# RMSNorm with SiLU on one core: later stores, earlier sums, one Newton step fewer, a square moved to ScalarE, and a halved last store

## The chip, the core and the metric

The kernel runs on one core of one Trainium2 chip. The metric is the device time of the program in microseconds (us). TensorE is called PE in the profile, VectorE DVE, ScalarE ACT, GpSimd POOL and SyncE SP. A load brings data from HBM into SBUF, a store takes it back. Loads are issued on the SP queue (row q1 of the page), stores on the ACT queue (q10), and the page counts the packets of both against the same 16 DMA engines: in the kernel before, loads alone took 100.0% of their time (12.84 to 32.27 us, 432 GB/s), stores alone 100.6% (290 to 302 us, 434 GB/s), and the two mixed 50.4% and 50.0% (42 to 280 us, 433 GB/s).

## The reference

The input `x` is 8 x 1024 rows of 2048 float32, `gamma` has 2048 values.

```python
rms = np.sqrt(np.mean(x ** 2, axis=-1, keepdims=True) + eps)
out = gamma * x / rms
return (out * (1 / (1 + np.exp(-out)))).astype(np.float32)
```

67.1 MB must be read and 67.1 MB written. Nothing can be kept back.

## The kernel before

The 8192 rows are cut into 16 blocks of 128 partitions x 4 rows, 4.19 MB each. Six buffers hold one block each; the load of block b+6 goes into the buffer of block b as soon as its store has landed. A block is squared and summed (two rows on ScalarE, two on VectorE), VectorE computes 1/rms by a bit trick and four Newton steps, multiplies by gamma, and ScalarE applies Silu with 1/rms as its scale.

```python
def rsqrt(ss):
    # ... var = ss / d + eps, then the first guess y by a shift and a subtraction
    for _ in range(4):
        nc.vector.scalar_tensor_tensor(out=t, in0=y, scalar=-0.5, in1=y, op0=ALU.mult, op1=ALU.mult)
        nc.vector.tensor_mul(out=t, in0=t, in1=var)
        nc.vector.scalar_tensor_tensor(out=y, in0=t, scalar=1.5, in1=y, op0=ALU.add, op1=ALU.mult)
    return y

def work(b):
    # ... rows 0 and 1: nc.scalar.activation(Square, accum_out=...)
    # ... rows 2 and 3: nc.vector.tensor_tensor_reduce(...)
    rstd = rsqrt(ss)
    for j in range(J):
        nc.vector.tensor_mul(out=row(b, j), in0=row(b, j), in1=g)
        nc.scalar.activation(out=row(b, j), in_=row(b, j), func=ACT.Silu, scale=rstd[:, j:j + 1])
    nc.scalar.dma_start(out=ob[b], in_=blocks.pop(b))

for b in range(nblk):
    work(b)
    if b + LEAD < nblk:      # LEAD = 6
        load(b + LEAD)       # on the SP queue; waits for the store of b
```

Of the kernel before, what the change touches and what calls it, by code (L numbers as in the profile page):

```python
# [1 line left out]

# [4 lines left out]

ACT = mybir.ActivationFunctionType
ALU = mybir.AluOpType


@with_exitstack
def kernel(
    ctx: ExitStack,
    tc: tile.TileContext,
    x: bass.AP,
    gamma: bass.AP,
    eps: bass.AP,
    out: bass.AP,
):  # L20





    nc = tc.nc
    P = nc.NUM_PARTITIONS
    f32, i32 = mybir.dt.float32, mybir.dt.int32
    x2 = x.flatten_outer_dims()
    o2 = out.flatten_outer_dims()  # L30
    n, d = x2.shape
    J = 4
    BUFS, LEAD = 6, 6
    nblk = n // (P * J)
    xb = x2.rearrange("(b p j) d -> b p (j d)", p=P, j=J)
    ob = o2.rearrange("(b p j) d -> b p (j d)", p=P, j=J)

    singles = ctx.enter_context(tc.tile_pool(name="singles", bufs=1))
    pool = ctx.enter_context(tc.tile_pool(name="pool", bufs=BUFS))
    small = ctx.enter_context(tc.tile_pool(name="small", bufs=2))  # L40
    psum = ctx.enter_context(tc.tile_pool(name="psum", bufs=1, space=bass.MemoryType.PSUM))

    g = singles.tile([P, d], f32)
    ones = singles.tile([1, P], f32)
    junk_a = psum.tile([P, d], f32, name="junk_a")
    junk_v = psum.tile([P, d], f32, name="junk_v")
    blocks = {}

    def load(b):
        xt = pool.tile([P, J * d], f32, name="xt")  # L50
        nc.sync.dma_start(out=xt, in_=xb[b])
        blocks[b] = xt

    def row(b, j):
        return blocks[b][:, j * d:(j + 1) * d]

    def rsqrt(ss):


        var = small.tile([P, J], f32, name="var")  # L60
        nc.vector.tensor_scalar(out=var, in0=ss, scalar1=1.0 / d, scalar2=float(eps),  # L61
                                op0=ALU.mult, op1=ALU.add)
        y = small.tile([P, J], f32, name="y")
        t = small.tile([P, J], f32, name="t")
        nc.vector.tensor_single_scalar(out=t.bitcast(i32), in_=var.bitcast(i32), scalar=1,  # L65
                                       op=ALU.logical_shift_right)
        nc.vector.tensor_scalar(out=y.bitcast(i32), in0=t.bitcast(i32), scalar1=-1, scalar2=0x5F375A00,  # L67
                                op0=ALU.mult, op1=ALU.add)
        for _ in range(4):
            nc.vector.scalar_tensor_tensor(out=t, in0=y, scalar=-0.5, in1=y, op0=ALU.mult, op1=ALU.mult)  # L70
            nc.vector.tensor_mul(out=t, in0=t, in1=var)  # L71
            nc.vector.scalar_tensor_tensor(out=y, in0=t, scalar=1.5, in1=y, op0=ALU.add, op1=ALU.mult)  # L72
        return y

    def work(b):
        ss = small.tile([P, J], f32, name="ss")
        for j in (0, 2, 1, 3):
            if j < J // 2:
                nc.scalar.activation(out=junk_a, in_=row(b, j), func=ACT.Square,  # L79
                                     accum_out=ss[:, j:j + 1])  # L80
            else:
                nc.vector.tensor_tensor_reduce(  # L82
                    out=junk_v, in0=row(b, j), in1=row(b, j), scale=1.0, scalar=0.0,
                    op0=ALU.mult, op1=ALU.add, accum_out=ss[:, j:j + 1])
        rstd = rsqrt(ss)
        for j in range(J):
            nc.vector.tensor_mul(out=row(b, j), in0=row(b, j), in1=g)  # L87
            nc.scalar.activation(out=row(b, j), in_=row(b, j), func=ACT.Silu, scale=rstd[:, j:j + 1])  # L88
        nc.scalar.dma_start(out=ob[b], in_=blocks.pop(b))  # L89

    with tc.manual_schedule():
        grow = pool.tile([P, J * d], f32, name="xt")
        nc.scalar.dma_start(out=grow[0:1, 0:d],
                            in_=bass.AP(tensor=gamma.tensor, offset=gamma.offset, ap=[[d, 1], gamma.ap[0]]))
        for b in range(min(LEAD, BUFS - 1)):
            load(b)
        nc.vector.memset(ones, 1.0)  # L97
        for c in range(0, d, 512):
            nc.tensor.matmul(junk_v[:, c:c + 512], ones, grow[0:1, c:c + 512], start=True, stop=True)  # L99
        nc.vector.tensor_copy(out=g, in_=junk_v)  # L100
        load(BUFS - 1)
        for b in range(nblk):
            work(b)
            if b + LEAD < nblk:
                load(b + LEAD)


# [1 line left out]
_INS = ['x', 'gamma', 'eps']  # L109
_OUTS = [((8, 1024, 2048), 'float32')]  # L110

_NUMBERS = {'eps': 9.999999747378752e-06}


# [26 lines left out]
```

## Time and profile before

| | before |
|---|---|
| time, median of 4 runs | 319.52 us (319.48 to 319.63) |
| span in the profile | 317.6 us |
| VectorE / ScalarE busy | 256.8 us (81%) / 194.8 us (61%) |
| DMA, both data queues | 98.5% of 16 engines' time |
| GB/s from 42 to 303 us | 433 |

The time is some 1.8 us longer than the span from the first to the last instruction. The groups of instructions of the page (line, engine, operation, form, count | busy us, mean ns of one | idle time before them and what ended it) give the unit costs:

```profile
L87 DVE TENSOR_TENSOR xt<-xt,g 128x2048 f32<-128x2048 f32 x64 | 142.2, 2284 | 0.0
L79 ACT ACTIVATE junk_a<-xt 128x2048 f32<-128x2048 f32 x32 | 60.2, 1881 | 17.1 <-DMA xt<-in_x_dram 10.3
L61 DVE TENSOR_SCALAR var<-ss 128x4 f32<-128x4 f32 x16 | 2.7, 170 | 27.9 <-ACT junk_a L79 27.8
```

The reader is to see that every large instruction costs about 2 us (1.88 to 2.30) for one row of 128 partitions, and that VectorE waits 27.8 us in all for ScalarE's squares. The lines that show what bounds the kernel stand in the prediction.

### The profile page before, as it was taken

To read this page: it belongs to the slowest core of one execution; us is meant where nothing else is said; L and a number is where in the kernel's file an instruction comes from. 1 tells how busy PE (TensorE), PEld (TensorE's weight loads), DVE (VectorE), ACT (ScalarE), POOL (GpSimd) and SP (SyncE) were. 2 spreads that over 40 slices of the span, in tenths; PEclk is the share of its full clock that TensorE was granted. 3 is DMA by queue.
4 is the path that set the end of the run, shared out by engine and by line. 5 is a ranking of instruction groups with operands and counts; after the bars stand their busy time and mean duration, and the time that the engine had idled before them with its cause. 6 is when DMAs were issued, how large, how long until landed. Compare 5 with 4: busy or idle time off the path is not lost.

```text
span 317.6 us, 637 instructions
## 1 busy us (share of the span) xinstructions
PE 7.2 (2%) x8; PEld 2.5 (1%) x8; DVE 256.8 (81%) x370; ACT 194.8 (61%) x130; POOL 0.2 (0%) x4
## 2 busy tenths in 40 slices
PE   6200000000000000000000000000000000000000
PEld 2000000000000000000000000000000000000000
DVE  0699697997979798897979799797979979797920
ACT  1339577483848659383956838395774838486540
POOL 0000000000000000000000000000000000000000
DMA  8999999999999999999999999999999999999967
GB/s 331 421 438 446 380 429 442 414 462 404 454 413 442 438 425 450 410 454 410 446 425 438 442 421 454 404 454 421 438 437 426 446 417 446 413 450 421 438 285 330
DMA packets 4614, 134.26 MB, mean 423 GB/s; under 512 B 513, under 2 KB 513, under 8 KB 513
## 3 DMA queue, kind: packets, MB, share of 16 engines
q1 hardware_dynamic: 2304, 67.11, 49.5%
q10 hardware_dynamic: 2306, 67.12, 49.0%
q14 instruction: 4, 0.03, 0.0%
HBM read 67.12 MB, written 67.11 MB: 423 GB/s over the span
## 4 chain that ended last, share of the span: by engine, by line
DVE 58%; ACT 27%; issue 4%; DMA 4%; ACTq 2%; DVEq 1%
DVE xt L87 44%; ACT junk_a L79 17%; ACT xt L88 10%; DMA xt<-in_x_dram 4%; DVE t L70 3%; DVE t L71 3%; DVE y L72 3%; ACTq L89 2%; DVE junk_v L82 1%; DVE t L65 1%; DVE var L61 1%; DVE y L67 1%; DVEq L136 1%; DVE ss L82 0%; DVEq L61 0%
## 5 line engine op out<-in xcount | busy, mean ns | idle before, releaser
L88 ACT ACTIVATE xt<-xt,y 128x2048 f32<-128x2048 f32 x64 | 128.1, 2002 | 92.5 <-DVE xt L87 92.3
L87 DVE TENSOR_TENSOR xt<-xt,g 128x2048 f32<-128x2048 f32 x64 | 142.2, 2284 | 0.0
L82 DVE CUSTOM_DVE_ANT_0 junk_v<-xt 128x2048 f32<-128x2048 f32 x32 | 73.5, 2296 | 1.3 <-DMA xt<-in_x_dram 0.8
L79 ACT ACTIVATE junk_a<-xt 128x2048 f32<-128x2048 f32 x32 | 60.2, 1881 | 17.1 <-DMA xt<-in_x_dram 10.3
L61 DVE TENSOR_SCALAR var<-ss 128x4 f32<-128x4 f32 x16 | 2.7, 170 | 27.9 <-ACT junk_a L79 27.8
L72 DVE SCALAR_TENSOR_TENSOR y<-t,y 128x4 f32<-128x4 f32 x64 | 10.4, 162 | 2.2
L70 DVE SCALAR_TENSOR_TENSOR t<-y 128x4 f32<-128x4 f32 x64 | 10.4, 162 | 2.2
L71 DVE TENSOR_TENSOR t<-t,var 128x4 f32<-128x4 f32 x64 | 10.3, 161 | 2.2
L100 DVE COPY g<-junk_v 128x2048 f32<-128x2048 f32 x1 | 2.3, 2291 | 8.9 <-PE junk_v L99 8.9
L99 PE MATMUL junk_v<-xt,ones 1*128 1x512 f32 x8 | 7.2, 1072 | 2.7 <-DMA xt<-in_gamma_dram 2.7
L79 ACT ACTIVATION_READ_ACCUMULATOR junk_a<-xt 128x1 f32 x32 | 6.0, 186 | 0.0
L82 DVE DVE_READ_ACCUMULATOR2_ANT ss<- 128x1 f32 x32 | 4.5, 140 | 0.0
L65 DVE TENSOR_SCALAR t<-var 128x4 int32<-128x4 int32 x16 | 2.7, 170 | 0.5
L67 DVE TENSOR_SCALAR y<-t 128x4 int32<-128x4 int32 x16 | 2.7, 170 | 0.5
L99 PEld LDWEIGHTS junk_v<-xt,ones 1*128 1x128 f32 x8 | 2.5, 325 | 5.8 <-issue 5.8
L79 ACT ACT_TABLE_LOAD x1 | 1.3, 1283 | 1.3 <-PEq L122 1.3
L88 ACT ACT_TABLE_LOAD x1 | 1.3, 1283 | 0.0
L97 DVE MEMSET ones<- 1x128 f32 x1 | 0.2, 165 | 0.8 <-PEq L122 0.8
L122 POOL MEMSET const-bfloat16-1.0<- 128x1 bf16 x1 | 0.1, 102 | 0.0
L122 POOL MEMSET const-uint8-127<- 128x1 uint8 x1 | 0.1, 102 | 0.0
L122 POOL MEMSET const-float32-1.0<- 128x1 f32 x1 | 0.1, 99 | 0.0
L122 POOL MEMSET const-float32-0.0<- 128x1 f32 x1 | 0.1, 98 | 0.2 <-issue 0.2
## 6 DMA issues: line engine op xcount, KB each, us to landing
xt<-in_x_dram SPq DMA_DIRECT2D x16, 4096.0 KB, 53.1
out_dram<-xt ACTq DMA_DIRECT2D x16, 4096.0 KB, 30.7
xt<-in_gamma_dram ACTq DMA_DIRECT2D x1, 8.0 KB
```

Source lines behind the costliest of these rows:

```text
L61: nc.vector.tensor_scalar(out=var, in0=ss, scalar1=1.0 / d, scalar2=float(eps), op0=ALU.mult, op1=ALU.add)
L65: nc.vector.tensor_single_scalar(out=t.bitcast(i32), in_=var.bitcast(i32), scalar=1, op=ALU.logical_shift_right)
L67: nc.vector.tensor_scalar(out=y.bitcast(i32), in0=t.bitcast(i32), scalar1=-1, scalar2=0x5F375A00, op0=ALU.mult, op1=ALU.add)
L70: nc.vector.scalar_tensor_tensor(out=t, in0=y, scalar=-0.5, in1=y, op0=ALU.mult, op1=ALU.mult)
L71: nc.vector.tensor_mul(out=t, in0=t, in1=var)
L72: nc.vector.scalar_tensor_tensor(out=y, in0=t, scalar=1.5, in1=y, op0=ALU.add, op1=ALU.mult)
L79: nc.scalar.activation(out=junk_a, in_=row(b, j), func=ACT.Square, accum_out=ss[:, j:j + 1])
L82: nc.vector.tensor_tensor_reduce(out=junk_v, in0=row(b, j), in1=row(b, j), scale=1.0, scalar=0.0, op0=ALU.mult, op1=ALU.add, accum_out=ss[ ...
L87: nc.vector.tensor_mul(out=row(b, j), in0=row(b, j), in1=g)
L88: nc.scalar.activation(out=row(b, j), in_=row(b, j), func=ACT.Silu, scale=rstd[:, j:j + 1])
L89: nc.scalar.dma_start(out=ob[b], in_=blocks.pop(b))
L99: nc.tensor.matmul(junk_v[:, c:c + 512], ones, grow[0:1, c:c + 512], start=True, stop=True)
```

## The change

Its intent: take work off VectorE, the busiest compute engine; sum a block before the Silu of the block ahead of it, so that neither engine waits for the other; hold a store back so that loads run ahead and stores are left over to cover the arithmetic of the last block; and begin the last store when half of the block is done. Cut to its core (`...` marks cuts):

```diff
-        for _ in range(4):
+        for _ in range(3):
 ...
-    def work(b):
+    def sums(b, after_first=()):
         ss = small.tile([P, J], f32, name="ss")
-        for j in (0, 2, 1, 3):        # two rows on each engine
+        ... row J-1 by nc.vector.tensor_tensor_reduce
+        for j in range(J - 1):
+            nc.scalar.activation(out=junk_a, in_=row(b, j), func=ACT.Square,
+                                 accum_out=ss[:, j:j + 1])
+            if j == 0:
+                for s in after_first:
+                    store(s)
 ...
+    def finish(b, pieces=1):
+        ... multiply and Silu row by row; with pieces=2 a store after two rows
+    def store(b):
+        nc.scalar.dma_start(out=ob[b], in_=blocks[b])
+        if b + LEAD < nblk:
+            load(b + LEAD)
 ...
-        for b in range(nblk):
-            work(b)
-            if b + LEAD < nblk:
-                load(b + LEAD)
+        sums(0); rstds[0] = rsqrt(sss[0]); finish(0)
+        sums(1); rstds[1] = rsqrt(sss[1])
+        for b in range(1, last - 1):
+            sums(b + 1, after_first=[b - 1])
+            finish(b)
+            rstds[b + 1] = rsqrt(sss[b + 1])
+        store(last - 2); finish(last - 1); store(last - 1)
+        sums(last); rstds[last] = rsqrt(sss[last])
+        finish(last, pieces=2)
```

More of the change, by code (lines that the diff above doesn't have):

```diff
@@ L46 @@
     junk_v = psum.tile([P, d], f32, name="junk_v")
-    blocks = {}
+    blocks, sss, rstds = {}, {}, {}
     def load(b):
@@ L73, in rsqrt @@
         return y
-    def work(b):
+    def sums(b, after_first=()):
         ss = small.tile([P, J], f32, name="ss")
-        for j in (0, 2, 1, 3):
-            if j < J // 2:
-                nc.scalar.activation(out=junk_a, in_=row(b, j), func=ACT.Square,
-                                     accum_out=ss[:, j:j + 1])
-            else:
-                nc.vector.tensor_tensor_reduce(
-                    out=junk_v, in0=row(b, j), in1=row(b, j), scale=1.0, scalar=0.0,
-                    op0=ALU.mult, op1=ALU.add, accum_out=ss[:, j:j + 1])
-        rstd = rsqrt(ss)
+        nc.vector.tensor_tensor_reduce(
+            out=junk_v, in0=row(b, J - 1), in1=row(b, J - 1), scale=1.0, scalar=0.0,
+            op0=ALU.mult, op1=ALU.add, accum_out=ss[:, J - 1:J])
+        for j in range(J - 1):
[4 more added lines that the diff above has]
+                    store(s)
+        sss[b] = ss
+    def finish(b, pieces=1):
         for j in range(J):
             nc.vector.tensor_mul(out=row(b, j), in0=row(b, j), in1=g)
-            nc.scalar.activation(out=row(b, j), in_=row(b, j), func=ACT.Silu, scale=rstd[:, j:j + 1])
-        nc.scalar.dma_start(out=ob[b], in_=blocks.pop(b))
+            nc.scalar.activation(out=row(b, j), in_=row(b, j), func=ACT.Silu,
+                                 scale=rstds[b][:, j:j + 1])
+            if pieces > 1 and (j + 1) % (J // pieces) == 0:
+                w = J // pieces * d
+                i = (j + 1) // (J // pieces) - 1
+                nc.scalar.dma_start(out=ob[b][:, i * w:(i + 1) * w], in_=blocks[b][:, i * w:(i + 1) * w])
+    def store(b):
+        nc.scalar.dma_start(out=ob[b], in_=blocks[b])
+        if b + LEAD < nblk:
+            load(b + LEAD)
     with tc.manual_schedule():
@@ L101 @@
         load(BUFS - 1)
-        for b in range(nblk):
-            work(b)
-            if b + LEAD < nblk:
-                load(b + LEAD)
+        last = nblk - 1
+        sums(0)
+        rstds[0] = rsqrt(sss[0])
+        finish(0)
+        sums(1)
+        rstds[1] = rsqrt(sss[1])
+        for b in range(1, last - 1):
+            sums(b + 1, after_first=[b - 1])
+            finish(b)
+            rstds[b + 1] = rsqrt(sss[b + 1])
+        store(last - 2)
+        finish(last - 1)
+        store(last - 1)
+        sums(last)
+        rstds[last] = rsqrt(sss[last])
+        finish(last, pieces=2)
 _INS = ['x', 'gamma', 'eps']
```

## The prediction

> **What bounds the kernel now.** I read the page's engine shares first, then the slices and the DMA part.
>
> ```profile
> PE 7.2 (2%) x8; PEld 2.5 (1%) x8; DVE 256.8 (81%) x370; ACT 194.8 (61%) x130; POOL 0.2 (0%) x4
> ...
> DMA  8999999999999999999999999999999999999967
> ...
> DMA packets 4614, 134.26 MB, mean 423 GB/s; under 512 B 513, under 2 KB 513, under 8 KB 513
> ...
> q1 hardware_dynamic: 2304, 67.11, 49.5%
> q10 hardware_dynamic: 2306, 67.12, 49.0%
> q14 instruction: 4, 0.03, 0.0%
> ```
>
> VectorE is busy 81% of the span, the two data queues together 98.5% of the DMA engines' time, and only the last two slices are below 9. The page's chain of work ends in VectorE's multiply (44%), but that is a chain through the engine that also happens to be just ahead of the DMA. The view of the stretches tells which resource is full (columns: stretch, length, busy of PE, PEld, DVE, ACT, POOL, clock, DMA share, GB/s):
>
> ```profile
> 42.00:280.00 238.00, 0.00 (x0) 0.00 (x0) 207.14 (x300) 156.76 (x105) 0.00 (x0) 1.00 1.00 433
> 280.00:303.00 23.00, 0.00 (x0) 0.00 (x0) 20.71 (x26) 16.35 (x11) 0.00 (x0) 1.00 1.00 433
> 303.00:304.00 1.00, 0.00 (x0) 0.00 (x0) 0.54 (x1) 0.80 (x2) 0.00 (x0) 1.00 0.08 33
> 304.00:305.00 1.00, 0.00 (x0) 0.00 (x0) 0.00 (x0) 1.00 (x1) 0.00 (x0) 1.00 0.08 33
> 305.00:306.00 1.00, 0.00 (x0) 0.00 (x0) 0.00 (x0) 0.58 (x1) 0.00 (x0) 1.00 0.08 33
> 306.00:316.00 10.00, 0.00 (x0) 0.00 (x0) 0.00 (x0) 0.00 (x0) 0.00 (x0) 1.00 0.98 419
> ```
>
> The reader is to see a DMA share of 1.00 and a flat 433 GB/s from 42 to 303 us, with loads and stores mixed in any proportion, and one hole from 303.6 to 306.5: the last Silu ends at 305.6, and only then is the last store issued. The waits say the same. The compute engines wait for a load only at the start, while the load queue waits 217 us for stores to free buffers:
>
> ```profile
> ACT junk_a L79 <- DMA xt<-in_x_dram: 10.3, 1, 10.3
> ...
> SPq L51 <- DMA out_dram<-xt: 217.3, 10, 45.7
> ```
>
> So **the kernel is DMA-bound**. 134.26 MB at 433 GB/s is 310.1 us of the 317.6. A load and a store of one block are 8.39 MB, 19.4 us at that rate; compute takes 18.3 us a block (multiplies of successive blocks start at 38.99 and 57.25).
>
> [...] pure loads (30 us) and pure stores (290 to 302 us) run at the same 433 as the mixture. [...] The four packets of the row "q14 instruction" are 8 KB each[...]. This matters below.
>
> **The straggler.** In the hole the DMA view moves 33 GB/s: one 32 KB packet starting in each microsecond. A packet lasts 1.213 us, so exactly one of 16 engines is still working. I chained the packet records end to start into 16 engines (the records don't name the engine, so this is a reconstruction). Fifteen chains stop between 303.3 and 304.3 and idle 2.2 to 3.3 us. One chain has no gap at all: it ends the store of block 14 at 306.5, starts the last store in the same instant, and all chains end between 316.2 and 316.4. On that chain lie three of the four instruction packets, at 56.7, 148.7 and 242.8 us; each takes 0.31 us and makes the data packet beside it 0.54 us longer: 0.85 each, 2.55 together. Between two of them VectorE has begun 121 to 124 further instructions (counts 70, 194, 315 of its 393 records)[...]. So I read them as the refill of VectorE's instructions. Another 0.5 us of that chain's lag comes from some slowed packets at 79 to 99 us, cause unknown. **The hole is therefore idle on fifteen engines but not on the one that ends the kernel**; closing it gains nothing by itself, since a store lands only when every engine has done its share.
>
> **The change part by part.**
>
> 1. *One square from VectorE to ScalarE.* VectorE loses one reduce per block, 2.296 us + 0.14 for reading the accumulator: 2.4 us. ScalarE gains 1.881 + 0.186, some 2.03 us in sequence. [...]
> 2. *Three Newton steps.* Three instructions fewer, 0.196 us from start to start: 0.6 us a block.
> 3. *Sums of b+1 in front of Silu of b.* The 1.9 us in which VectorE waits for ScalarE's squares before each rsqrt (27.8 us over 15 blocks) disappears, as the sums are done a block earlier.
>    Sum: VectorE 4 x 2.22 + 2.45 + 12 x 0.2 = 13.7 us a block; ScalarE 3 x 2.03 + 4 x 2.02 + 0.4 for the issue = 14.6 us. Compute falls from 18.3 to 14.6 us a block. None of it is on the path: the DMA needs 19.4.
> 4. *Stores held back until block b+2 has landed.* A delay of a store delays the reuse of its buffer, which could starve the load queue. I walked it through: loads 0 to 2 land at 12.8, 22.5 and 32.3 (trace). The store of 0 goes out at about 34, load 3 lands near 48, then one load every 19.4 us. When load k is in flight, two further loads are queued or about to be, because store k-4 ends 7 us after load k-1 landed. So the DMA queue always holds over one block of work, and no bubble is expected. Compute of block b ends 14.6 us after block b+1 has landed, before the 19.4 at which its store is due.
> 5. *The end.* Load 15 lands at about 281 instead of 284. Left then are 2.35 blocks of stores (a third of 12, then 13 and 14), 22.8 us, so fifteen engines run dry at about 304 as before. Store 13 is issued near 276, store 14 near 286.5. Squares of 15 run to 293, rsqrt to 295.7, first half stored at 302.3 (two multiplies and a Silu later) with first bytes 0.85 later: 303.2, just before the queue is dry. Second half: issued at 306.9, needed at 308.6. The hole closes, from 2.7 us to about nothing.
>
> What ends the kernel is the straggling engine: first byte at 1.9, slow start 0.7, 256 packets of 1.213 less overlap = 309.8, the slow packets around the first store (33 to 36 us) 0.7, hence 313.1 without disturbance; plus 0.85 for each refill. Before: 3 refills + 0.6 of others = 316.3, as measured. After: VectorE's 393 records shrink by 16 x (2 + 3) = 80 to 313, and the third refill came at record 315, so probably two remain. 313.1 + 1.7 + 0 to 0.6 = 314.8 to 315.4. From the last packet to the end of the span are 1.3 us (316.3 to 317.6), from the span to the measured time 1.9 (317.6 to 319.5): 318.0 to 318.6. With a third refill, 318.8 to 319.4.
>
> **The rivals.** (a) *The hole is the loss*: the aggregate rate, not one engine, counts, or the straggler's delay is an accident of this execution. Then 2.75 us are gained: 316.8. For it speaks that DMA is 1.00 everywhere else; against it the one chain without a gap. (b) *Compute is the bound*, as the page's chain has it. Then 3.6 us a block would be gained, some 50 us; against it stands the flat 433 GB/s, which no reordering raises. (c) *The held-back stores starve the loads* or the last compute: a hole of 5 to 10 us, 323 to 328. Against it speak over one block of backlog, and the slack of 5 us between the end of block b's compute and its store. (d) *Half stores cost*: 16 KB packets and one more completion[...], hidden in the range.
>
> **Range and chances.** Faster by 2% means under 313.1 us. Even with no refill and no hole the sum is 313.1 + 1.3 + 1.9 = 316.3, so that is practically excluded: 0.01. Slower by 2% needs (c): 0.01. I put the value at 318.3, between two refills and three, and the range from 317.3 (rival a in part) to 319.4 (three refills, nothing gained).
>
> **What would show it.** In the changed kernel: DMA share 1.00 with 433 GB/s from about 42 to over 310 us, and no 33 GB/s stretch near 304; instead a thin tail at the very end, in which fifteen engines are done and one still moves packets. The row "q14" with fewer VectorE refills. VectorE busy near 215 us and ScalarE near 227, both with long waits for loads: first squares of a block waiting on the DMA some 4 to 5 us each. If the last slices fall to zero without a thin tail and the time is 316.8, the straggler was no bound. If a hole stands in the middle or around 304 to 308, step 4 or 5 is wrong.

That neither loads nor stores nor their mixture run faster than the others is read from the trace alone (432, 434 and 433 GB/s, as given above); that the q14 packets are refills was the reading of the counts of instructions.

## The result, and the profile after

| | before | after |
|---|---|---|
| time, median of 4 runs | 319.52 us | 319.05 us (317.89 to 319.27) |
| span in the profile | 317.6 us | 317.5 us |
| VectorE busy | 256.8 us (81%) | 210.3 us (66%) |
| ScalarE busy | 194.8 us (61%) | 221.3 us (70%) |
| VectorE records in the trace | 393 | 313 |

The ratio is 0.9977 with a 95% interval of 0.9953 to 1.0002: the same within 2%. Ratios are the mean time of one kernel's fast runs over that of the other's of the same rounds, so not quite the ratio of the medians. The four runs of the changed kernel are not spread evenly: 319.27, 319.22 and 318.88 on one side, 317.89 on the other, while the four of the kernel before lie within 0.15 us. In the later rounds the kernel before spreads from 319.27 to 320.67 us, with medians of 319.56 to 319.74, so a small difference is best taken from the ratio, which compares runs of the same rounds. Every run below is "the same" by the 2% measure, but for squares3, which has no verdict; what follows is about differences of some tenths of a per cent.

The page of the changed kernel, engines, DMA and the row q14:

```profile
PE 7.2 (2%) x8; PEld 2.5 (1%) x8; DVE 210.3 (66%) x290; ACT 221.3 (70%) x162; POOL 0.2 (0%) x4
...
DMA  8999999999999999999999999999999999999994
...
q14 instruction: 4, 0.03, 0.0%
```

46.5 us of VectorE's work are gone, and the span is 0.1 us shorter. The last slice but one, 6 before, is now 9: the hole is closed. But the last slice fell from 7 to 4. The view of the stretches shows why (columns as in the prediction):

```profile
280.00:303.00 23.00, 0.00 (x0) 0.00 (x0) 12.39 (x18) 15.39 (x11) 0.00 (x0) 1.00 1.00 433
...
306.00:312.00 6.00, 0.00 (x0) 0.00 (x0) 0.00 (x0) 0.00 (x0) 0.00 (x0) 1.00 1.02 437
312.00:313.00 1.00, 0.00 (x0) 0.00 (x0) 0.00 (x0) 0.00 (x0) 0.00 (x0) 1.00 0.99 426
313.00:314.00 1.00, 0.00 (x0) 0.00 (x0) 0.00 (x0) 0.00 (x0) 0.00 (x0) 1.00 0.20 82
314.00:315.00 1.00, 0.00 (x0) 0.00 (x0) 0.00 (x0) 0.00 (x0) 0.00 (x0) 1.00 0.08 33
315.00:316.00 1.00, 0.00 (x0) 0.00 (x0) 0.00 (x0) 0.00 (x0) 0.00 (x0) 1.00 0.08 33
```

The flat rate now runs on to 313 us, and then 33 GB/s remain. A packet of the last store is 16 KB and takes 0.61 us; two of them start in each microsecond, so one DMA engine works and fifteen are done. **The hole of 2.7 us has moved from in front of the last store to behind it.** The waits say that compute has become slack:

```profile
ACT junk_a L83 <- DMA xt<-in_x_dram: 64.0, 11, 10.6
DVE junk_v L79 <- DMA xt<-in_x_dram: 57.5, 11, 6.4
DVE var L61 <- ACT junk_a L83: 15.7, 3, 6.3
```

Before, ScalarE waited once for a load, 10.3 us; now both engines wait for most blocks.

### The profile page after: what moved, and what is told of

It is laid out like the page before. It is cut to its first block, busy times and chain, and to the rows that moved or that the text cites. A ratio compares the mean times of both kernels' runs of the same rounds, so it can differ in the third digit from the quotient of the medians.

```text
span 317.5 us, 603 instructions
## 1 busy us (share of the span) xinstructions
PE 7.2 (2%) x8; PEld 2.5 (1%) x8; DVE 210.3 (66%) x290; ACT 221.3 (70%) x162; POOL 0.2 (0%) x4
## 4 chain that ended last, share of the span: by engine, by line
DMA 73%; DVE 11%; ACT 7%; issue 3%; DVEq 1%; ACTq 0%; SPq 0%
DMA xt<-in_x_dram 39%; DMA out_dram<-xt 34%; DVE xt L92 8%; ACT junk_a L83 5%; ACT xt L93 3%; DVE junk_v L79 1%; DVEq L164 1%; DVE t L70 0%; DVE t L71 0%; DVE y L72 0%; DVE t L65 0%; DVE y L67 0%; DVE var L61 0%; ACTq L98 0%; ACTq L101 0%
## 5 line engine op out<-in xcount | busy, mean ns | idle before, releaser
L83 ACT ACTIVATE junk_a<-xt 128x2048 f32<-128x2048 f32 x48 | 90.3, 1881 | 65.5 <-DMA xt<-in_x_dram 64.0
L93 ACT ACTIVATE xt<-xt,y 128x2048 f32<-128x2048 f32 x64 | 124.0, 1992 | 13.0 <-DVE xt L92 13.0
L79 DVE CUSTOM_DVE_ANT_0 junk_v<-xt 128x2048 f32<-128x2048 f32 x16 | 36.8, 2299 | 57.5 <-DMA xt<-in_x_dram 57.5
L83 ACT ACTIVATION_READ_ACCUMULATOR junk_a<-xt 128x1 f32 x48 | 9.0, 187 | 0.0
L72 DVE SCALAR_TENSOR_TENSOR y<-t,y 128x4 f32<-128x4 f32 x48 | 7.8, 162 | 1.7
L70 DVE SCALAR_TENSOR_TENSOR t<-y 128x4 f32<-128x4 f32 x48 | 7.8, 162 | 1.7
L71 DVE TENSOR_TENSOR t<-t,var 128x4 f32<-128x4 f32 x48 | 7.8, 162 | 1.6
L79 DVE DVE_READ_ACCUMULATOR2_ANT ss<- 128x1 f32 x16 | 2.3, 142 | 0.0
```

The source lines that it names most:

```text
L79: nc.vector.tensor_tensor_reduce(out=junk_v, in0=row(b, J - 1), in1=row(b, J - 1), scale=1.0, scalar=0.0, op0=ALU.mult, op1=ALU.add, accum ...
L83: nc.scalar.activation(out=junk_a, in_=row(b, j), func=ACT.Square, accum_out=ss[:, j:j + 1])
```

## The experiments

**How the lag is measured.** The trace holds 16 completion signals for each load and each whole or half store of a block, with the time of each. They are read as one from each DMA engine: in the traces of the kernel before and of the changed one, the 16 signals of the last transfer, put in order, follow the ends of the 16 chains described below by 0.33 to 0.50 us each. What waits for a transfer goes on after the last signal: in the kernel before, the signals of the store of block 0 came from 54.36 to 55.96 us, half of them by 54.53, and the load that needed its buffer was issued at 56.03. The last signal of a transfer less the median of its 16 is here called the lag. This was worked out from the completion records, since no view of the profile names a DMA engine. For each fast profiled execution whose end is free of a hole, the lag of the very last transfer stands beside the time of that same execution; in the kernel before all engines end together after the hole (the last 16 signals lie within 0.17 us), so its lag is given at the store before the last. "Refills", the prediction's word, are here the 8 KB packets of the row "q14 instruction" that are put down to VectorE. No trace shows what such a packet carries; that it brings VectorE its instructions is the reading of the row's name and of the number of instructions that each engine had begun. In the kernel before VectorE had begun 70, 194 and 315 at three of the four packets, in the changed kernel 45 and 178 at two of the four, so 121 to 133 apart; the others are put down to ScalarE, which had begun 67 in the kernel before, 67 and 191 in the changed one. The packets were also chained end to start into 16 engines, as in the prediction; where the text speaks of chains, it rests on that reconstruction.

```
kernel      VectorE records  refills  last signal  lag   time of this execution
before            393           3       316.71     (*)   319.35
after             313           2       316.56     2.76  319.27
again             313           2       315.33     1.44  318.05
newton3           345           3       316.19     2.27  318.85
oldsplit          393           3       316.06     2.27  318.77
nohold            313           2       316.84     2.92  319.55
whole             313           2       316.66     2.85  319.31
newton8           553           4       317.31     3.54  320.02
few               137           1       314.57     0.90  317.28
sqrt              135           1       316.60     2.49  319.31
first4            135           1       315.38     0.70  318.17
(*) at the store before the last: 3.12
```

Time less last signal is 2.64 to 2.79 us in every line. The median engine's last signal (last signal less lag) lies at 313.7 to 314.1 us in all lines from "after" to "sqrt", and at 314.7 in the last. So **time = about 316.5 us + lag**, and the experiments can be read as changes of the lag.

### 1. Closing the hole alone

```diff
 # the kernel before
-        for _ in range(4):
+        for _ in range(3):
```

> The kernel before with three Newton steps in place of four, nothing else. VectorE's round falls from 18.27 to 17.7 us, so the last Silu ends some 9 us sooner and the last store is issued before the DMA engines run dry near 304 us: the hole of 303.6 to 306.5 us closes. Theory (one lagging DMA engine ends the kernel): the hole was idle time of fifteen engines only, so 319.0 to 319.6 us, and a thin tail of one engine stands at the end. Rival (the hole was the loss): about 316.8 us.

Measured: 318.85 us (318.83 to 318.89, 4 runs), ratio 0.9970 (0.9957 to 0.9983). The stretches at the two places in question:

```profile
303.00:304.00 1.00, 0.00 (x0) 0.00 (x0) 0.00 (x0) 0.00 (x0) 0.00 (x0) 1.00 1.22 524
304.00:305.00 1.00, 0.00 (x0) 0.00 (x0) 0.00 (x0) 0.00 (x0) 0.00 (x0) 1.00 0.46 197
...
314.00:315.00 1.00, 0.00 (x0) 0.00 (x0) 0.00 (x0) 0.00 (x0) 0.00 (x0) 1.00 0.08 33
```

The hole is all but gone: in the chains, 12 of the 16 engines still idle 0.2 to 0.7 us before the last store, where 15 idled 2.2 to 3.3 before (a packet of 1.2 us is counted where it starts, which exaggerates the 524 and the 197). The thin tail stands at the end. The hole was closed and 0.7 us came out (0.9 against the median of the kernel before in the same rounds, 319.74), not the 2.7 of the rival. The theory holds in kind; its number, 319.0 at the least, was 0.15 us too high. One deleted Newton step gained about as much as the whole change: its ratio lies between the 0.9977 and the 0.9959 of the two rounds of the changed kernel. The two traced executions differ by 0.50 us (319.35 and 318.85), and this is accounted for to 0.02 us: at the store before the last the lag was 3.12 us in the kernel before and 2.73 here, and the median engine was 0.13 us earlier. What makes the lag smaller is not shown.

### 2. The changed kernel once more

The kernel is unaltered.

> The changed kernel once more, unaltered, for its spread and for a second trace. Theory (lag of one engine, partly chance): times between 317.8 and 319.4 us, differing with the size of the lag of the last engine behind the median one at the end (2.76 us in the first trace, at a time of 319.3). Rival (a fixed engine is slow in the same way each time): the same time within 0.2 us and the same lag.

Measured: 318.05, 319.08, 318.14, 319.04, 318.23 and 317.97 us, on chip 3; ratio 0.9959 (0.9944 to 0.9974). With the first four runs that makes ten in two clusters, five from 317.89 to 318.23 and five from 318.88 to 319.27. The profiled execution fell in the lower one, and its tail is shorter:

```profile
313.00:314.00 1.00, 0.00 (x0) 0.00 (x0) 0.00 (x0) 0.00 (x0) 0.00 (x0) 1.00 0.24 98
314.00:315.00 1.00, 0.00 (x0) 0.00 (x0) 0.00 (x0) 0.00 (x0) 0.00 (x0) 1.00 0.12 49
315.00:316.00 1.00, 0.00 (x0) 0.00 (x0) 0.00 (x0) 0.00 (x0) 0.00 (x0) 1.00 0.00 0
```

The lag is 1.44 us in place of 2.76, a difference of 1.32; the times differ by 1.22. The rival, a fixed slow engine, falls. The packet records point to the accident, in these two traced executions. As the first store begins, at 40 to 42 us, nearly every DMA engine has one load packet of 1.5 to 1.9 us in place of 1.213. In the first trace one engine had a packet of 2.98 us there, 1.76 too long; counted at the stores, the lag of the last engine over the median jumps from 0.3 to 2.4 us at that place and stays about there or above. In the second trace the longest such packet is 2.58 us. The engine with the two VectorE refills lags by 1.30 us at the end of the first trace and is only the second to last.

### 3. A small store ahead of the first

```diff
 # the changed kernel
         nc.vector.tensor_copy(out=g, in_=junk_v)
+        nc.scalar.dma_start(out=ob[nblk - 1][:, 0:256], in_=g[:, 0:256])
```

> The changed kernel with one small store (1 KB for each partition, 128 KB) to the last block's output issued at about 12 us, long before the first real store; the last block's store overwrites it. Theory (the first store of a program costs something of its own: packets of 1.7 to 3.0 instead of 1.21 us on all engines as it starts, and one engine got 1.76 us of lag from it): the slow packets move to 12 us or vanish, the lag of the last engine is under 1.5 us, time 317.0 to 318.5 us. Rival (slow packets come with any onset of mixed loads and stores, or from the size of the store): slow packets remain at 40 us, time as the changed kernel, 319.

Measured: three fast runs of 318.19, 318.24 and 318.02 us, and three slow ones of 324.27, 326.06 and 331.0. The ratio of the fast runs is 0.9948 (0.9934 to 0.9963). The trace fell in a slow run, in which packets were long in many places, so no difference is read from it; but load packets of 1.5 to 2.2 us stand at 40 to 43 us in it as well, so the burst at the first large store did not move to 12 us. The three fast runs are all in the lower cluster, which is too few to call a gain. The theory of a price of the first store as such finds no support here; the run is inconclusive.

### 4. The square moved without the new order

```diff
 # the kernel before, with three Newton steps
-        for j in (0, 2, 1, 3):
-            if j < J // 2:
+        for j in (0, 3, 1, 2):
+            if j < J - 1:
```

> The kernel before with three rows squared on ScalarE and three Newton steps, but sums still behind Silu of the block before. Then one block is squares 6.1 + rsqrt 2.4 + multiplies 8.9 + last Silu 2.2 + issue 0.4, 20.0 us in a row, more than the DMA's 19.4: the kernel becomes bound by that chain, 12.9 + 16 x 20.0 + 12 = 345 us. Rival (compute is never on the path, the DMA bounds whatever the order): 319 us.

Measured: 341.74 us in one look, whose state is unknown. Two successive blocks in the timeline:

```profile
159.33 8.89 DVE L87 TENSOR_TENSOR xt<-xt,g 128x2048 f32<-128x2048 f32 x4
...
179.04 8.89 DVE L87 TENSOR_TENSOR xt<-xt,g 128x2048 f32<-128x2048 f32 x4
```

A block takes 19.71 us from multiply to multiply, where 20.0 were expected and the DMA needs 19.4, and compute becomes the bound. So this part of the change does harm without the new order of the sums; with it, in the changed kernel and in nohold and whole, it does none.

### 5 and 6. More and fewer VectorE instructions

```diff
 # newton8: the changed kernel
-        for _ in range(3):
+        for _ in range(8):
```

> The changed kernel with eight Newton steps in place of three: 240 more tiny instructions on VectorE (553 records in place of 313), 3 us more a block, still 16.7 us against the DMA's 19.4. Theory (each refill of VectorE's instructions costs the same one DMA engine some 0.9 us, and the last engine ends the kernel): two more refills, some 4 in all, the last engine lags the median one by 3.2 to 4.2 us at the end, time 319.8 to 320.8 us. Rival (refills are noise, the lag comes only from the first store): 318.1 to 319.3 us as the changed kernel.

Measured: 319.8 us (319.51 to 320.02, 4 runs). Its tail:

```profile
314.00:315.00 1.00, 0.00 (x0) 0.00 (x0) 0.00 (x0) 0.00 (x0) 0.00 (x0) 1.00 0.08 33
315.00:316.00 1.00, 0.00 (x0) 0.00 (x0) 0.00 (x0) 0.00 (x0) 0.00 (x0) 1.00 0.08 33
316.00:317.00 1.00, 0.00 (x0) 0.00 (x0) 0.00 (x0) 0.00 (x0) 0.00 (x0) 1.00 0.04 16
```

```diff
 # few: the changed kernel, a straight line in place of the whole rsqrt
+        nc.vector.tensor_scalar(out=y, in0=ss, scalar1=-0.5 / d, scalar2=1.5,
+                                op0=ALU.mult, op1=ALU.add)
```

> The changed kernel with the rsqrt replaced by one instruction, a straight line through the sum of squares (the result is wrong on purpose by some tenths of a per cent or more): VectorE's records fall from 313 to about 137. Theory: one refill on VectorE in place of two, so that engine's lag is 0.4 to 0.6 us; the time is then set by the lag from the first store (0.4 to 1.8 us by chance): 317.2 to 318.7 us, median under 318.1. Rival (no part played by refills): 318.1 to 319.1 in two clusters as the changed kernel.

Measured: 317.24 us (317.11 to 317.9, 6 runs), ratio 0.9926 (0.9913 to 0.9939). It passed the comparison with the reference only because these rows have a mean square near 1; it is a probe, not a kernel. Its tail:

```profile
313.00:314.00 1.00, 0.00 (x0) 0.00 (x0) 0.00 (x0) 0.00 (x0) 0.00 (x0) 1.00 0.12 49
314.00:315.00 1.00, 0.00 (x0) 0.00 (x0) 0.00 (x0) 0.00 (x0) 0.00 (x0) 1.00 0.00 0
```

Both kernels ran in the same rounds on the same chip and bracket the changed kernel: four refills 319.8 us, one refill 317.24, 2.56 us for three refills, 0.85 us each. That this equals the price read from the packets (0.31 + 0.54) is in part chance: in the chains of few, the last engine is one with ScalarE's two refills and 0.88 us of lag, and the engine with VectorE's refill lags by 0.67. In both, compute is slack (13.7 + 3 us a block at the most, estimated from the prediction's sum, against 19.4), so the tiny instructions are off the path as work. What the traces show beside them is a q14 packet of 0.31 us and, right behind it, a data packet of about 1.75 (1.60 to 1.86) in place of 1.213. The refills of VectorE strike the same DMA engine each time, as far as the lag of the last engine can tell: in newton8 it stands at 1.3, 2.3, 3.2 and 4.1 us before and after the refills of 102.6, 167.6 and 236.3 us (every other transfer, those that land at 99, 120, 198 and 238 us), and settles at 3.54. In the trace of newton3 the lag of the last engine rises by 0.96 us at the refill of 164 us and by 0.97 at that of 274 us. In the chains, all VectorE refills of a trace lie on one chain in the seven traces that have two or three of them. The rival, refills as noise, falls.

### 7. The Newton steps on GpSimd

```diff
 # the changed kernel; multiplies also joined to two rows each
-            nc.vector.scalar_tensor_tensor(... three instructions a step ...)
+            nc.gpsimd.tensor_mul(out=t, in0=y, in1=y)
+            nc.gpsimd.tensor_mul(out=t, in0=t, in1=var)
+            nc.gpsimd.tensor_scalar(out=t, in0=t, scalar1=-0.5, scalar2=1.5, op0=ALU.mult, op1=ALU.add)
+            nc.gpsimd.tensor_mul(out=y, in0=y, in1=t)
```

> The changed kernel with the Newton steps moved to GpSimd and two rows to a multiply: the right result with about 150 records on VectorE and 220 on GpSimd. Theory: VectorE has one refill, GpSimd one or two, and if these strike different DMA engines no engine has over 1 us of lag from them: 317.3 to 318.5 us. Rival (GpSimd's tiny instructions are slow or hold up VectorE, or its refills strike the same engine): 318 to 320 us.

Measured: 325.5 us (325.34 to 325.75, 4 runs), ratio 1.018 (1.0165 to 1.0195). The lag is gone, 0.1 us at the end, but a new wait took its place. The waits:

```profile
ACT xt L98 <- POOL y L73: 50.0, 7, 18.0
```

and the stretches in front of the last store:

```profile
305.00:310.00 5.00, 0.00 (x0) 0.00 (x0) 0.00 (x0) 2.22 (x2) 1.97 (x10) 1.00 0.58 249
```

Silu waited 50 us for GpSimd, up to 18 us for one block, so the last half store was issued at 316 us instead of 301 and the DMA engines ran at 249 GB/s there. Here the hole is real idle time of all 16 engines, 3.3 to 4.9 us in the chains, 4.1 in the mean. It is not the whole loss: the median engine ends 9.0 us later than in the changed kernel (322.8 and 313.8), and some 3.5 us of that are four further bursts of slow packets between 70 and 110 us, which the changed kernel does not have. The theory's time missed by 7 us; the rival's reason (slow GpSimd instructions) was right and its time too low.

### 8, 9 and 10. The other parts of the change, one undone at a time

```diff
 # nohold: the changed kernel
-            sums(b + 1, after_first=[b - 1])
+            sums(b + 1)
             finish(b)
+            store(b)
```

> The changed kernel with each store issued as soon as its Silu is done, not held until block b+2 has landed. Theory (reordering stores against loads makes no bandwidth): first store near 26 us instead of 38, flat 433 GB/s, the end unchanged, 317.9 to 319.4 us. Rival (the hold is what hides the last block's compute): load 15 lands later, a hole appears before the last store, 320 to 323 us.

Measured: 318.57 us (317.93 to 319.55, 4 runs), ratio 0.9965 (0.9945 to 0.9985). No hole in front of the last store; the first store went out at 32.3 us, not at 26, because ScalarE was busy until then. The spread is that of the changed kernel. In its trace no packet at the first store is over 2.1 us; two refills and a row of load packets that were 0.1 to 0.3 us too long, after 160 us, brought one engine to a lag of 2.92.

```diff
 # oldsplit: the changed kernel with the arithmetic of the kernel before
-        for _ in range(3):
+        for _ in range(4):
 ...
-        # row J-1 on VectorE, rows 0 to J-2 on ScalarE
+        # rows J//2 to J-1 on VectorE, rows 0 to J//2-1 on ScalarE
```

> The changed kernel with the arithmetic of the kernel before: two rows squared on each engine, four Newton steps (about 393 VectorE records, three refills); the new order of sums, the held stores and the halved last store stay. VectorE needs 16.8 us a block, under the DMA's 19.4. Theory (new order and held stores gain nothing; what the change gains is one refill fewer on one DMA engine, 0.9 us): 318.8 to 319.5 us, lag of the last engine 2.3 to 3.2 us. Rival (the new order or the held stores carry the gain): 318.1 to 318.5.

Measured: 318.78 us (318.65 to 319.0, 5 runs), ratio 0.9971 (0.9956 to 0.9985), lag 2.27 us. Both lie just under the foot of the theory's ranges (318.8 and 2.3). Here three refills set the lag and the spread is small; not one of five runs came under 318.65, where five of ten of the changed kernel did. So the new order, the held stores and the halves without the lighter arithmetic do what one Newton step fewer did (318.85): they close the hole.

```diff
 # whole: the changed kernel
-        finish(last, pieces=2)
+        finish(last)
+        store(last)
```

> The changed kernel with the last store in one piece. Its issue is at about 301.1 us, still ahead of the 303.6 at which the engines would run dry. Theory: no difference, 317.9 to 319.3 us in the same two clusters. Rival (the halves close the hole): 319.5 or more, with a hole near 304 us.

Measured: 318.07 us (317.91 to 319.31, 4 runs), ratio 0.9956 (0.9936 to 0.9975): the two clusters again, 317.91 to 318.19 and 319.31. No effect of the halves is seen. The profiled execution, the 319.31, has one packet of 3.23 us at 41.5 us, the longest of any trace, and a lag of 2.85.

### 11. A right kernel with few VectorE instructions

```diff
 # the changed kernel; epst is a [P, 1] tile that holds eps
-        ... shift, subtraction and three Newton steps
+        nc.scalar.activation(out=root, in_=ss, func=ACT.Sqrt, scale=1.0 / d, bias=epst)
+        nc.vector.reciprocal(out=y, in_=root)
```

> The changed kernel with a right rsqrt in few VectorE instructions: square root on ScalarE (two table loads of 1.28 us a block, ScalarE some 17.3 us a block) and a reciprocal on VectorE, about 137 VectorE records and one refill. Theory: as the kernel with the straight line, 317.1 to 318.0 us, faster than the kernel before by 0.5 to 0.8 per cent, the best right result. Rival (ScalarE's table loads put it on the path or its own refills, now at two or three, strike one engine): 318 us or more.

Measured: 317.65 us (317.39 to 319.31, 7 runs), ratio 0.9932 (0.9919 to 0.9946), result right. **By its median this is the best right kernel**, 0.7% faster than the kernel before: six of seven runs lie from 317.39 to 317.88. The seventh, 319.31, is the one that was profiled:

```profile
313.00:314.00 1.00, 0.00 (x0) 0.00 (x0) 0.00 (x0) 0.00 (x0) 0.00 (x0) 1.00 0.54 229
314.00:315.00 1.00, 0.00 (x0) 0.00 (x0) 0.00 (x0) 0.00 (x0) 0.00 (x0) 1.00 0.42 180
315.00:316.00 1.00, 0.00 (x0) 0.00 (x0) 0.00 (x0) 0.00 (x0) 0.00 (x0) 1.00 0.27 115
```

ScalarE is busy 84%, below the DMA (98.7%), and no cost of its table loads (33 of 1.28 us) is seen. In this execution several engines are late, two of them by 2.5 us, with lags already at 1.7 us at the transfer that landed at 63 us, before any refill (the first is at 77.6). So fewer instructions take away one source of lag and leave the other.

### 12. The first store in four

```diff
 # sqrt, with the store of block 0 in four, one row each
+        n_parts = 4 if b == 0 else 1
+        w = J * d // n_parts
+        for i in range(n_parts):
+            nc.scalar.dma_start(out=ob[b][:, i * w:(i + 1) * w], in_=blocks[b][:, i * w:(i + 1) * w])
```

> The kernel with the square root on ScalarE, with the first store in four stores of one row each (8 KB packets), nothing else. If the slow packets at the first store (1.6 to 3.2 us in place of 1.21, some 2 us after its issue) come from the size of that one store, they shrink, and no run has the long lag: 317.2 to 317.7 us throughout. If they come with the onset of stores beside loads whatever the size, they stay, and times spread over 317.4 to 319.3 us as without the split.

Measured: 317.73 us (317.3 to 318.32, 6 runs), ratio 0.9938 (0.9926 to 0.995). No run over 318.4, but no better than the unsplit one within the intervals. In its trace the slow packets at the first store are few and short (1.5 to 1.6 us at 40 us), seven packets of about 1.6 us stand at 64 us, and a larger burst of up to 2.4 us at 84 to 86 us, some 14 us after the issue of block 2's store; it slowed nearly all engines alike, so the median engine ended at 314.7. The burst was moved, not removed. What makes it stays open.

## Why the prediction was right

The predicted 318.3 us was 0.75 us under the measured 319.05, within its range of 317.3 to 319.4. (It calls 318.3 "between two refills and three"; by its own sum it is the middle of the range for two.) The number owes something to chance: in the first trace the engine that ended the kernel carried no refill. By its own steps:

- **What bounds the kernel** was right. 46.5 us less work on VectorE moved the time by 0.5 us, and the rate stayed at 431 to 433 GB/s. Undoing the lighter arithmetic (oldsplit) moved it just as little. Rival (b), compute as the bound, fell; it holds only where the order of the sums makes a block longer than 19.4 us (squares3, 341.74).
- **The straggler** was right in kind, and it is what kept the gain small. The predicted thin tail stands at the end of the trace. Rival (a), that the hole is the loss and 316.8 us come out, fell with newton3: the hole all but closed and 0.7 us gained. Its other half, that the lag is an accident of one execution, is partly true: the slow packet under "the mis-sized term" below is such an accident. A count of the idle share of all engines would have promised 2.7.
- **The refills**: two on VectorE were predicted, at some 120 records' distance, and two came, at 49.2 and 168.6 us, 133 records apart. Each was put at 0.85 us; newton8 against few gives 0.85, in part by chance, and the lag in newton3 rises by 0.96 at each.
- **The mis-sized term** is the one for the slow packets around the first store, "0.7", put on the straggler as on every other engine. It measured 0.5 to 1.8 us from engine to engine: one engine got a packet of 2.98 us in the first trace and so a lag of 2.76, overtaking the engine with the refills, which was at 1.30. With the lag of the engine with the refills alone the predicted 318.0 to 318.6 is what half of the runs show (317.89 to 318.23); the other half are at 318.88 to 319.27. That such a packet sets the cluster is seen in the traced executions alone (after, again, whole); for the runs without a trace it is not shown. The prediction gave one value where there are two.
- **The end** was right in its outcome (no hole) and early events were off by some 5 us: the first store was issued at 38.5 us, not 34, as ScalarE was still squaring block 1; loads so ran further ahead, load 15 landed at 276.6 by its last signal instead of 281 (and at 285.3 in the kernel before, where the prediction read 284), and the halves went out at 296.7 and 301.1 us instead of 302.3 and 306.9. The slack of 0.8 us that the prediction found (303.2 against 304) was in truth one of 6.
- **Compute per block** was right: VectorE 210.3 us busy against 215 predicted, ScalarE 221.3 against 227. The waits of ScalarE's first squares were 5.3 us each (64.0 less the first block's 10.6, over 10) where 4 to 5 were expected.
- **Rivals (c) and (d)**: no bubble from held stores, and the halves cost nothing that could be seen (whole).

Three things stay open. What makes the burst of slow packets as the first large stores begin: a small store ahead did not move it and a split one moved it later. The chains hold a hint: the slow packet of an engine is mostly its last load packet before its first store packet (in the changed kernel on 15 of 16 engines), and in pool2 the same stands on all 16 engines where stores set in again after loads alone (81 us) and loads after stores alone (98 us). Whether it is the change between loads and stores that costs, no run tests. What makes the small delays of 0.1 to 0.4 us on single packets that add to one engine's lag (79 to 99 us in the kernel before, after 160 us in nohold). And what makes the lag of newton3 0.4 us smaller than that of the kernel before, with as many refills.

## What to carry to other kernels

When transfers fill all DMA engines, a hole in the aggregate rate is not yet a loss: ask whether the engine that ends last is idle in it. Here the hole was 2.7 us, and closing it alone gained 0.7 (newton3). A transfer was complete only with the last of its 16 signals, at the end of the kernel up to 3.54 us after the median one (newton8), so in this DMA-bound kernel the end was set by whatever disturbed one DMA engine, and that was in part as small a thing as the number of instructions on VectorE. Once compute was off the path, more or less work on VectorE moved the time little (oldsplit 0.9971 against 0.9977 and 0.9959 for the changed kernel), and the right kernel with the fewest VectorE instructions was the best (sqrt, 0.9932).
